# GpSimd leaves the decode and the first MLP groups; P·V takes score banks

## The chip, the cores and the metric

The kernel runs on one core of a Trainium2 chip. The metric is device time in microseconds (us) of one launch. A core has engines with instruction queues of their own that meet only through semaphores: PE (TensorE, matrix products), DVE (VectorE, elementwise work), ACT (ScalarE, activations and copies), POOL (GpSimd) and SP (SyncE, which here issues most DMAs). Each queue runs in program order, so an instruction that waits holds all that stands behind it.

## The reference

One layer of a decoder with attention and short convolution side by side, for a prompt of 512 tokens and for 8 decoded sequences of one token each. All is float32.

```python
h = rmsnorm(x); q, k, v, vc, gate_b, gate_c = split(h @ w_in)      # 2048 -> 6 x 1024
q, k = rmsnorm per head (64 wide, 16 heads)
o    = merge of 3 dilated branches (window, step) (128,1) (512,4) (2048,16), T5 bias
y    = gate_b * conv3(gate_c * vc)
x   += [rmsnorm(o) || rmsnorm(y)] @ w_out
x   += relu(rmsnorm(x) @ w_up)^2 @ w_down                          # 2048 -> 8192 -> 2048
```

For the prompt the three branches lie in the same 512 tokens and become one table of logit biases per head. For the decode a token reads a cached window of 2048 keys and values, of which 128, 96 and 96 rows (plus the new one) are used. The outputs are x of both, the new keys and values, and the rolled caches.

## The kernel before

**Numbers and layout.** The 520 tokens lie as two halves of 260 columns. A product is made from three matmuls in a reduced float32 format (fp32r): the weight's high part by x's high part, high by low, low by high. A weight tile of 128x1024 comes by DMA (`raw`), ScalarE copies its high part (`whi`, L148 or L789), VectorE subtracts for the low part (`wlo`, L149 or L790). So each weight tile needs a DMA, ScalarE and VectorE before TensorE may use it; a split is issued while the half before it is at work.

**Stages.** (1) To 36 us the first pass over x: per k-tile ScalarE and VectorE make high and low parts (`split_act`, L288 and L289) and sums of squares (L310, L311), while TensorE does the q and k of head pair 0. The bias products (L334, L335) stand ahead of it: a one-hot table by the bucket table, plus a mask `lc`. (2) To 430 us the q, k, v projections, a half of a weight column (48 matmuls) at a time. `block()` calls `step()` after every third matmul; a step advances two background generators: `norm_gen` (norm of q and k, L405 to L417) and `attn_gen` (attention of head pair j while the projections of j+1 run). (3) To 708 us the convolution's projections with `dec_gen`, the decode, as the background: a K stage (24 items of one sequence and one branch: multiply by q, reduce over the head), softmax, and a V stage (24 items: multiply by the weights, add over the branches, sum over positions by a matmul with the selector `sel`). (4) To 880 us the output projection with sums for the MLP's operands (`pair_a`, `pair_b`) and the sum of squares `acc2`. (5) To 1525 us the MLP up in 32 groups and then the MLP down in 32 groups, each group 7 products in Strassen's manner, of 24 matmuls a weight. A group's weight quarters (o, h) are combined by four sums (`SUMS`, `q_sum`), on GpSimd or VectorE as `on_vector` says. `q_prep(n)` loads, sums and splits ahead of product n; `late_gen` makes the last three operands T3, B22 and T4 while the first products run.

**PSUM banks.** Matmul outputs live in pools: `mm` for projections, `pw` (`wtile()`, 2 banks) for transposes, norms and P·V, `pS` (`stile()`, 2 banks) for scores. A pool with two banks makes the third user wait until the first is read out.

**Attention.** `products` and `score` (logits plus bias, maximum, exponential) for four blocks of queries; `norm_p` divides; `trans(hp, tb)` transposes P by TensorE (L476) into a `pw` bank, ScalarE and VectorE read it into high and low parts (L479, L480); `pv(hp)` multiplies with V (L486) into another `pw` bank and then adds two halves (L491, L492).

**What sets the order.** Every engine works in the order in which the program issues its instructions; the `wait(n)` of a generator, n steps, sets where in that order its work stands. These lines are the ones that the change touches most:

```python
P.tensor_tensor(t[:NP[g], 8 * i:8 * i + 8], ..., tiles["q", b, i][:NP[g]], OP.mult)      # K stage, L600
yield from wait(7)
V.tensor_reduce(sc[:NP[g], g, b * H:(b + 1) * H], t[:NP[g]], axis=AX.X, op=OP.add)       # L606
(V if g else P).tensor_tensor(t[:NP[g]], t[:NP[g]], w[:, :, None].to_broadcast(...), OP.mult)   # V stage, L660
T.matmul(od[m // 2], sel[:, 127 - b:255 - b], t, ...)                                    # L677
P.tensor_tensor(acc2, acc2, sq, OP.add)                                                  # L920
```

Of the kernel before, what the change touches and what calls it, by code (L numbers as in the profile page):

```python
# [25 lines left out]
F32 = mybir.dt.float32  # L26
# [58 lines left out]
def hymba_kernel(ctx, tc, xT, wi, wo, wu, wd, state_k, state_v, sconv, relb, relrep, ohp, lcp, ohd, lcd,  # L85
# [246 lines left out]
    for t in range(2):  # L332
        st = wtile()
        T.matmul(st[:H, :320], relt, oh[:, t * 320:(t + 1) * 320], start=True, stop=True)  # L334
        V.tensor_tensor(rr[:, t * 320:(t + 1) * 320], st[:H, :320], lc[:, t * 320:(t + 1) * 320], OP.add)  # L335
# [10 lines left out]
    for k in range(KT):  # L346
# [12 lines left out]
        elif k == 5:  # L359
# [3 lines left out]
            load(6)  # L363
        elif k == 9:
# [57 lines left out]
    def attn_gen(j):  # L422
# [59 lines left out]
        def pv(hp):  # L482
            st = wtile()
# [74 lines left out]
    def dec_gen():  # L558
# [36 lines left out]
        for n in range(len(items) + 1):  # L595
            if n < len(items):
                b, g = items[n]
                t = tiles["k", b, g]
                for i in range(2):
                    P.tensor_tensor(t[:NP[g], 8 * i:8 * i + 8], t[:NP[g], 8 * i:8 * i + 8],  # L600
                                    tiles["q", b, i][:NP[g]], OP.mult)
            yield from wait(7)
# [6 lines left out]
        yield from wait(6)  # L609
# [41 lines left out]
        od = [wtile(), wtile()]  # L651
# [3 lines left out]
        for n in range(len(items) + 1):  # L655
            if n < len(items):
# [3 lines left out]
                (V if g else P).tensor_tensor(t[:NP[g]], t[:NP[g]], w[:, :, None].to_broadcast([NP[g], H, E]), OP.mult)  # L660
            yield from wait(6)
            if n and items[n - 1][1]:
# [3 lines left out]
                if g == 2:  # L666
                    a = tiles.pop(("v", b, 0)).rearrange("p h e -> p (h e)")
                    parts = []
                    for i in range(2):
                        ah, al = (wk.tile([128, 512], F32R, name="ah", tag="w", bufs=16) for _ in range(2))  # L670
                        S.activation(ah, a[:, i * 512:(i + 1) * 512], AF.Copy)
                        V.tensor_tensor(al, a[:, i * 512:(i + 1) * 512], ah.bitcast(F32), OP.subtract)
                        parts += [ah, al]
                    prev(n + 2)
                    yield from wait(13)
                    for m, t in enumerate(parts):
                        T.matmul(od[m // 2], sel[:, 127 - b:255 - b], t, start=b == 0 and m % 2 == 0,  # L677
                                 stop=b == NB - 1 and m % 2 == 1)
            prev(n + 2)
            yield from wait(3)  # L680
        os = [wt((NB, 512), name="os") for _ in range(2)]
        for i in range(2):
            S.activation(os[i], od[i][:NB], AF.Copy)
        yield from wait(4)
        st = wtile()
        for f in range(8):
            T.transpose(st[:, f * NB:(f + 1) * NB], os[f // 4][:, f % 4 * 128:f % 4 * 128 + 128], ident[:NB, :NB])
        yield from wait(2)
        S.activation(R3.rearrange("p k a b -> p k (a b)")[:, :, SEQ:],
                     st[:, :64].rearrange("p (f b) -> p f b", f=8), AF.Copy)  # L690
# [113 lines left out]
    Q = {}  # L804

    def q_load(gi, o, h):
# [271 lines left out]
    for n in range(7 * NG):  # L1078
# [18 lines left out]
        if kind == "up":  # L1097
# [28 lines left out]
            if gi == 2 and pi == 4:  # L1126
# [5 lines left out]
                V.tensor_tensor(rstd2sq, rstd2, rstd2, OP.mult)  # L1132
# [123 lines left out]
```

## Time and profile before

| | us |
|---|---|
| median of 3 runs (lowest, highest) | 2200.83 (2197.87, 2202.15) |
| profiled execution, and its span | 2199.76, 2198.0 |
| PE busy | 2145.2 (98%) |
| DVE busy | 1790.6 (81%) |
| ACT busy | 965.4 (44%) |
| POOL busy | 233.3 (11%) |

The span runs from the first to the last instruction that the profiler records; 1.76 us of the profiled execution lie around it. Busy times of engines overlap, so they don't add up to the span. A row of a timeline has the start, the length in us, the engine, the line, the operation, the tile written and the tiles read with their shape, how many instructions the row stands for, and in square brackets how long the engine idled ahead of it and what ended that. "PEclk" is the granted clock of TensorE as a share of its full 2.4 GHz.

### The profile page before, as it was taken

The numbers are of one execution on the slowest core, as the hardware profiler recorded it, in microseconds if no ns is written. First come the engines' busy times: TensorE is split into PE (matmuls) and PEld (weight loads), VectorE is DVE, ScalarE is ACT, GpSimd is POOL, SyncE is SP. The second block draws the span as 40 slices with busy tenths as digits, with TensorE's granted clock in tenths as the row PEclk, the third lists the DMA queues.
The fourth block names the chain that finished last, engine by engine and source line by source line (L and its number), as shares of the span: only waits on it lengthen the run. The fifth ranks groups of instructions, "written<-read, shape, count | busy, mean of one in ns | idle before, by whom it ended". The sixth has DMA issues, their size and how long they took to land.

```text
span 2198.0 us, 42395 instructions
## 1 busy us (share of the span) xinstructions
PE 2145.2 (98%) x17568; PEld 2115.9 (96%) x17568; DVE 1790.6 (81%) x2355; ACT 965.4 (44%) x1391; POOL 233.3 (11%) x174
## 2 busy tenths in 40 slices
PE   8999999999999999899999999999999999999999
PEld 7888989998999999899999999999999999999999
DVE  6777766687787657988888888888999999999997
ACT  5444444312223334544444444445544444444443
POOL 1011010166120003630000000001100000000000
PEclk9999999999999999999999999999999999999999
DMA  5354443476544646547776676677886666666653
GB/s 197 130 171 139 170 153 111 125 219 208 169 156 160 220 171 222 202 153 243 251 247 216 235 251 232 230 254 258 319 291 246 233 247 225 237 239 247 232 195 127
DMA packets 137074, 457.75 MB, mean 208 GB/s; under 512 B 19409, under 2 KB 49745, under 8 KB 130481
## 3 DMA queue, kind: packets, MB, share of 16 engines
q1 hardware_dynamic: 136320, 454.81, 59.4%
q8 instruction: 138, 2.26, 0.4%
q14 instruction: 56, 0.45, 0.1%
q10 hardware_dynamic: 560, 0.22, 0.0%
HBM read 412.21 MB, written 181.16 MB: 270 GB/s over the span
## 4 chain that ended last, share of the span: by engine, by line
PE 85%; DVE 7%; DMA 3%; ACT 2%; issue 1%; POOL 1%; SPq 0%; DVEq 0%; ACTq 0%; POOLq 0%
PE mn L1023 28%; PE mm L1023 28%; PE mm L213 25%; DMA kv<-state_k 1%; DMA raw<-wi 1%; PE pS L453 1%; DVE wlo L790 1%; PE pw L476 1%; PE pw L486 1%; DVE wlo L149 1%; POOL kv L600 1%; DVE sc L606 1%; DVE R L790 1%; DVE raw L412 0%; PE pw L677 0%
## 5 line engine op out<-in xcount | busy, mean ns | idle before, releaser
L213 PE MATMUL mm<-R,whi 128*128 128x260 f32 x4000 | 678.1, 287 | 0.9 <-DVE R L289 0.9
L213 PEld LDWEIGHTS mm<-R,whi 128*128 128x128 f32 x4000 | 562.7, 190 | 11.6 <-issue 5.3
L1023 PE MATMUL mm<-R,whi 128*128 128x260 f32 x3008 | 549.6, 283 | 1.8 <-DVE R L790 1.2
L1023 PE MATMUL mn<-R,whi 128*128 128x260 f32 x3008 | 548.2, 283 | 0.0
L1023 PEld LDWEIGHTS mm<-R,whi 128*128 128x128 f32 x3008 | 464.9, 189 | 2.2 <-DVE R L790 1.5
L1023 PEld LDWEIGHTS mn<-R,whi 128*128 128x128 f32 x3008 | 463.7, 188 | 0.1
L1023 PE MATMUL mn<-R,wlo 128*128 128x260 f32 x1504 | 425.5, 283 | 6.3 <-DVE wlo L790 6.3
L1023 PE MATMUL mm<-R,wlo 128*128 128x260 f32 x1504 | 425.9, 283 | 5.4 <-DVE wlo L790 5.4
L213 PE MATMUL mm<-R,wlo 128*128 128x260 f32 x2000 | 404.8, 284 | 1.8 <-DVE wlo L149 1.8
L790 DVE TENSOR_TENSOR wlo<-raw,whi 128x1024 fp32r<-128x1024 f32 x255 | 319.1, 1252 | 104.9 <-ACT whi L789 103.4
L789 ACT ACTIVATE whi<-raw 128x1024 fp32r<-128x1024 f32 x255 | 269.3, 1056 | 209.6 <-PE mn L1023 95.0
L213 PEld LDWEIGHTS mm<-R,wlo 128*128 128x128 f32 x2000 | 310.7, 190 | 2.7 <-DVE wlo L149 2.2
L789 ACT ACTIVATE whi<-rg 128x1024 fp32r<-128x1024 f32 x186 | 197.3, 1061 | 219.5 <-PE mn L1023 90.1
L1023 PEld LDWEIGHTS mn<-R,wlo 128*128 128x128 f32 x1504 | 283.3, 188 | 7.8 <-DVE wlo L790 7.8
L1023 PEld LDWEIGHTS mm<-R,wlo 128*128 128x128 f32 x1504 | 284.2, 189 | 5.8 <-DVE wlo L790 5.8
L790 DVE TENSOR_TENSOR wlo<-rg,whi 128x1024 fp32r<-128x1024 f32 x186 | 230.8, 1241 | 1.7 <-ACT whi L789 1.7
L149 DVE TENSOR_TENSOR wlo<-raw,whi 128x1024 fp32r<-128x1024 f32 (+1 forms) x129 | 161.1, 1250 | 41.8 <-ACT whi L148 41.7
L148 ACT ACTIVATE whi<-raw 128x1024 fp32r<-128x1024 f32 (+1 forms) x129 | 133.5, 1038 | 128.6 <-PE mm L213 76.7
L600 POOL TENSOR_TENSOR kv<-kv,qb 128x512 f32<-128x512 f32 (+2 forms) x48 | 75.2, 1598 | 32.7 <-DMA kv<-state_k 32.7
L841 DVE TENSOR_TENSOR rg<-rg,raw 128x1024 f32<-128x1024 f32 x60 | 73.0, 1217 | 0.0
L841 DVE TENSOR_TENSOR raw<-rg,raw 128x1024 f32<-128x1024 f32 x58 | 71.1, 1225 | 2.0
L1145 DVE TENSOR_TENSOR yacc<-mm,yacc 128x520 f32<-128x520 f32 x96 | 66.6, 693 | 7.4 <-PE mm L1023 6.4
(234 smaller groups left out, 2483.2 us busy)
## 6 DMA issues: line engine op xcount, KB each, us to landing
oks<-state_k SPq DMA_DIRECT2D x184, 356.0 KB
ovs<-state_v SPq DMA_DIRECT2D x184, 356.0 KB
raw<-wi SPq DMA_DIRECT2D x94, 512.0 KB
raw<-wu SPq DMA_DIRECT2D x64, 512.0 KB
rg<-wd SPq DMA_DIRECT2D x64, 512.0 KB
raw<-wd SPq DMA_DIRECT2D x64, 512.0 KB
rg<-wu SPq DMA_DIRECT2D x60, 512.0 KB
raw<-wo SPq DMA_DIRECT2D x32, 512.0 KB
```

The source lines that it names most:

```text
L148: S.activation(his[i][:, h], raws[i][:, h], AF.Copy)
L149: V.tensor_tensor(los[i][:, h], raws[i][:, h], his[i][:, h].bitcast(F32), OP.subtract)
L213: T.matmul(ps[t][:, :HT] if isinstance(ps, tuple) else ps[:, t, :HT], a[:, k, :], b[:, t, :], start=start and n == 0, stop=stop and n == 2)
L453: T.matmul(ss[hp][:, :w], a[r, q], b[r, :w], start=n == 0, stop=n == 2)
L476: T.transpose(st[:, s * 128:(s + 1) * 128], lg[:, s * 128:(s + 1) * 128], ident)
L486: T.matmul(st[:, s * 128:], vv[:, hp, s].rearrange("p c e -> p (c e)"), b[:, s, s * 128:], start=s == 0 and n == 0, stop=s == 3 and n == 1 ...
L600: P.tensor_tensor(t[:NP[g], 8 * i:8 * i + 8], t[:NP[g], 8 * i:8 * i + 8], tiles["q", b, i][:NP[g]], OP.mult)
L789: S.activation(hi, src, AF.Copy)
L790: eng.tensor_tensor(lo, src, hi.bitcast(F32), OP.subtract)
L841: e.tensor_tensor(o_, a_, b_, op)
L1023: T.matmul(ps[:, r, :HT], a[:, k, :], b(kt), start=n % 7 in ((0, 1, 3) if kts == 8 else (0, 1)) and kt == 0 and m == 0, stop=kt == kts - 1 ...
L1145: V.tensor_tensor(dst[:, r], v[:, r], dst[:, r], OP.add)
```

## The change

Eight edits stand in it. The bias products move from ahead of the first pass into it, after tiles 7 and 8. P·V uses `stile()`. The K stage's multiplies and the V stage's g = 0 multiplies go from GpSimd to VectorE, and waits are 8 for 7, 12 for 6, and 10 for 13. The sum over positions takes the unsplit fp32 tile, in four strips of 32 PSUM partitions of one bank with 256 columns each, so `sel` is 64 wide; two 128x128 transposes follow where eight small ones did. For MLP groups 0 to 3, sum 1 is done by a DMA that adds as it writes (`accum_op`), on GpSimd's queue; the other sums of these groups, the `acc2` adds and all of `late_gen` go to VectorE, B22 in two pieces. The late squares of groups 0 to 2 become one VectorE instruction, with ScalarE's square one product later, and `rstd2sq` goes.

```diff
-    sel = cst.tile([128, 256], F32R, name="sel")
...
+    sel = cst.tile([128, 64], F32, name="sel")
+    V.memset(sel, 0.0)
+    V.memset(sel[:, 31:32], 1.0)
...
-    for t in range(2):
+
+    def bias_rows(t):
         st = wtile()
         T.matmul(st[:H, :320], relt, oh[:, t * 320:(t + 1) * 320], start=True, stop=True)
         V.tensor_tensor(rr[:, t * 320:(t + 1) * 320], st[:H, :320], lc[:, t * 320:(t + 1) * 320], OP.add)
...
+        elif k in (7, 8):
+            bias_rows(k - 7)
...
         def pv(hp):
-            st = wtile()
+            st = stile()
...
-                    P.tensor_tensor(t[:NP[g], 8 * i:8 * i + 8], t[:NP[g], 8 * i:8 * i + 8],
+                    V.tensor_tensor(t[:NP[g], 8 * i:8 * i + 8], t[:NP[g], 8 * i:8 * i + 8],
                                     tiles["q", b, i][:NP[g]], OP.mult)
-            yield from wait(7)
+            yield from wait(8)
...
-        yield from wait(6)
+        yield from wait(12)
...
-        od = [wtile(), wtile()]
+
+        od = wtile()
...
-                (V if g else P).tensor_tensor(t[:NP[g]], t[:NP[g]], w[:, :, None].to_broadcast([NP[g], H, E]), OP.mult)
+                V.tensor_tensor(t[:NP[g]], t[:NP[g]], w[:, :, None].to_broadcast([NP[g], H, E]), OP.mult)
...
-                    parts = []
-                    for i in range(2):
-                        ah, al = (wk.tile([128, 512], F32R, name="ah", tag="w", bufs=16) for _ in range(2))
-                        S.activation(ah, a[:, i * 512:(i + 1) * 512], AF.Copy)
-                        V.tensor_tensor(al, a[:, i * 512:(i + 1) * 512], ah.bitcast(F32), OP.subtract)
-                        parts += [ah, al]
+                    yield from wait(10)
+                    for c in range(4):
+                        T.matmul(od[32 * c:32 * c + 32, :256], sel[:, 31 - b:63 - b], a[:, 256 * c:256 * c + 256],
+                                 start=b == 0, stop=b == NB - 1, skip_group_check=True)
                     prev(n + 2)
-                    yield from wait(13)
-                    for m, t in enumerate(parts):
-                        T.matmul(od[m // 2], sel[:, 127 - b:255 - b], t, start=b == 0 and m % 2 == 0,
-                                 stop=b == NB - 1 and m % 2 == 1)
...
+    ADDED = 4
...
+        if (o, h) == (1, 0) and gi < ADDED:
+
+            a22 = groups[gi][3][1, 1]
+            if gi < 2:
+                for i in range(2):
+                    P.dma_start(Q[gi, o, h][i], a22[:, 4 * i:4 * i + 4], accum_op=OP.add)
+            else:
+                P.dma_start(t, a22, accum_op=OP.add)
...
-            return gi >= 4
+            return True
...
-        if gi < NG:
+        if gi < NG and not (i == 1 and gi < ADDED):
...
-            P.tensor_tensor(acc2, acc2, sq, OP.add)
+            V.tensor_tensor(acc2, acc2, sq, OP.add)
...
-        for i in range(4):
-            split2(XO["B22"][0][:, 2 * i:2 * i + 2], XO["B22"][1][:, 2 * i:2 * i + 2], R3[:, 2 * i:2 * i + 2, 1], P if i in (3,) else V)
-            yield from wait(5)
+        for i in range(2):
+            split2(XO["B22"][0][:, 4 * i:4 * i + 4], XO["B22"][1][:, 4 * i:4 * i + 4], R3[:, 4 * i:4 * i + 4, 1])
+            yield from wait(10)
...
-            split2(t4[:, 0, 2 * i:2 * i + 2], t4[:, 1, 2 * i:2 * i + 2], xs[i][:, :, 1], P if i in (1, 2, 3) else V)
+            split2(t4[:, 0, 2 * i:2 * i + 2], t4[:, 1, 2 * i:2 * i + 2], xs[i][:, :, 1])
...
         if late:
-            V.tensor_tensor(t, t, rstd2sq, OP.mult)
-        else:
-            S.activation(t, t, AF.Square)
+            V.scalar_tensor_tensor(t, t, 0.0, rstd2, op0=OP.max, op1=OP.mult)
+            relu.append(partial(square_out, t, k, n))
+            return
+        S.activation(t, t, AF.Square)
...
-                    V.scalar_tensor_tensor(t, t, 0.0, t, op0=OP.max, op1=OP.mult)
```

Three places show how the instructions move. First VectorE's queue in the decode's K stage. Before, reduces of the items (`sc<-kv`) and low parts of weights alternate:

```order
L149 TENSOR_TENSOR wlo<-raw,whi 128x1024
L606 TENSOR_REDUCE sc<-kv 97x16
L149 TENSOR_TENSOR wlo<-raw,whi 128x1024
L606 TENSOR_REDUCE sc<-kv 96x16
L700 TENSOR_TENSOR vc<-mm,rstd 128x520
L606 TENSOR_REDUCE sc<-kv 128x16
```

In the changed kernel the same stretch holds the multiplies by q as well:

```order
L149 TENSOR_TENSOR wlo<-raw,whi 128x1024
L603 TENSOR_TENSOR kv<-kv,qb 97x512 x2
L609 TENSOR_REDUCE sc<-kv 128x16
L603 TENSOR_TENSOR kv<-kv,qb 96x512 x2
L149 TENSOR_TENSOR wlo<-raw,whi 128x1024
L609 TENSOR_REDUCE sc<-kv 97x16
L603 TENSOR_TENSOR kv<-kv,qb 128x512 x2
```

Ahead of each reduce now stand two multiplies of the next item, and a weight's low part stands behind them.

Second TensorE's queue at P·V of head pair 1 (L486 before, L489 after; L476 and L479 are the transposes of the other head). Before:

```order
L486 MATMUL pw_2203<-R2_77 128x512 x2
L213 MATMUL mm_2179<-R0_75,whi_2010 128x260 x3
L486 MATMUL pw_2203<-R2_77 128x384 x2
L213 MATMUL mm_2179<-R0_75,whi_2010 128x260
L213 MATMUL mm_2179<-R0_75,wlo_2011 128x260 x2
L486 MATMUL pw_2203<-R2_77 128x256 x2
L213 MATMUL mm_2179<-R0_75,whi_2010 128x260 x3
L486 MATMUL pw_2203<-R2_77 128x128 x2
L213 MATMUL mm_2179<-R0_75,whi_2010 128x260
L213 MATMUL mm_2179<-R0_75,wlo_2011 128x260 x2
L213 MATMUL mm_2179<-R0_75,whi_2010 128x260 x3
L476 MATMUL pw_2235<-ident_114,R3_78 128x128
```

and in the changed kernel:

```order
L489 MATMUL pS_2203<-R2_77 128x512 x2
L213 MATMUL mm_2179<-R0_75,whi_2010 128x260 x3
L489 MATMUL pS_2203<-R2_77 128x384 x2
L213 MATMUL mm_2179<-R0_75,whi_2010 128x260
L213 MATMUL mm_2179<-R0_75,wlo_2011 128x260 x2
L489 MATMUL pS_2203<-R2_77 128x256 x2
L213 MATMUL mm_2179<-R0_75,whi_2010 128x260 x3
L489 MATMUL pS_2203<-R2_77 128x128 x2
L213 MATMUL mm_2179<-R0_75,whi_2010 128x260
L213 MATMUL mm_2179<-R0_75,wlo_2011 128x260 x2
L213 MATMUL mm_2179<-R0_75,whi_2010 128x260 x3
L479 MATMUL pw_2235<-ident_114,R3_78 128x128
```

The order is the same; only the bank of P·V is another, so that the transposes use both `pw` banks in turn.

Third, GpSimd's queue at the start of the MLP (`rw` and `rg` are weight quarters, `raw` too; T4x and R pieces of operands). Before:

```order
L841 TENSOR_TENSOR rw<-rw 128x512 x2
L920 TENSOR_TENSOR acc_9095<-acc_9095,sq 128x520
L841 TENSOR_TENSOR raw<-rw,raw 128x512 x2
L920 TENSOR_TENSOR acc_9095<-acc_9095,sq 128x520
L841 TENSOR_TENSOR rw<-rw,raw 128x512 x2
L841 TENSOR_TENSOR raw<-raw 128x1024
L841 TENSOR_TENSOR rw<-rw 128x512 x2
L790 TENSOR_TENSOR R_75<-R_78,R_75 128x520
L790 TENSOR_TENSOR T4x<-x_8030,T4x 128x520
```

and in the changed kernel, up to its last sums:

```order
L826 DMA rw<-wu 128x512 x4
L828 DMA rg<-wu 128x1024 x2
L848 TENSOR_TENSOR raw<-rg,raw 128x1024
L848 TENSOR_TENSOR raw<-raw 128x1024
L848 TENSOR_TENSOR rg<-rg 128x1024
```

The sums and the operand pieces are gone from this queue; six accumulating transfers stand in it, and the sums behind them belong to the end of the MLP up.

## Rows read from the trace of the kernel before

**Rows 1.** Windows: length; busy and count of PE, PEld, DVE, ACT, POOL; clock; DMA share, GB/s.

```profile
60.00:430.00 370.00, 351.98 (x2817) 332.68 (x2816) 258.89 (x621) 170.89 (x359) 33.88 (x32) 1.00 0.42 142
444.00:535.00 91.00, 89.19 (x741) 88.78 (x739) 76.51 (x66) 18.10 (x19) 69.79 (x56) 1.00 0.73 222
530.00:560.00 30.00, 25.60 (x185) 24.41 (x185) 18.22 (x24) 6.66 (x12) 8.46 (x10) 0.89 0.48 159
700.00:880.00 180.00, 180.00 (x1497) 179.88 (x1496) 123.71 (x168) 68.84 (x109) 22.75 (x17) 1.00 0.59 202
880.00:970.00 90.00, 77.47 (x599) 75.71 (x598) 81.13 (x75) 43.63 (x71) 52.81 (x24) 0.94 0.45 162
1000.00:1500.00 500.00, 500.00 (x4169) 500.00 (x4168) 418.09 (x499) 238.51 (x324) 0.00 (x0) 1.00 0.69 239
```

**Rows 2.** Waits of PE: who waits, for whom, us in total, times, longest.

```profile
PE pw L476 <- DVE R L492: 5.7, 7, 1.6
...
PE pw L476 <- DVE h L411: 5.1, 4, 1.3
```

**Rows 3.** Timeline of 0 to 10 us, all engines.

```profile
7.68 1.42 ACT L288 ACTIVATE R<-xt,g_all 128x520 fp32r<-128x520 f32 x2
...
8.79 0.88 DVE L335 TENSOR_TENSOR rr<-pw,lc 16x320 f32<-16x320 f32 x2 [6.58 <-DMA lc<-lcp]
```

**Rows 4.** Timeline of 34 to 40 us, PE.

```profile
35.95 1.58 PE L282 MATMUL pw<-acc,ones_d 128*128 128x260 f32 x6 [0.82 <-DVE acc L311]
37.17 0.83 PE L213 MATMUL mm<-R,whi 128*128 128x260 f32 x4
```

**Rows 5.** Timeline of 300 to 345 us, PE.

```profile
324.45 0.33 PE L476 MATMUL pw<-ident,R 128*128 128x128 f32 x1 [1.28 <-DVE h L411]
...
326.75 0.44 PE L476 MATMUL pw<-ident,R 128*128 128x128 f32 x2 [0.54 <-DVE R L492]
...
328.48 0.49 PE L476 MATMUL pw<-ident,R 128*128 128x128 f32 x3
```

**Rows 6.** Timeline of 312 to 336 us, DVE.

```profile
326.73 0.29 DVE L480 TENSOR_TENSOR R<-pw,R 128x128 fp32r<-128x128 f32 x1
```

**Rows 7.** Groups by line, POOL: busy us, mean ns, idle before and its releasers.

```profile
L600 POOL TENSOR_TENSOR kv<-kv,qb 128x512 f32<-128x512 f32 (+2 forms) x48 | 75.2, 1598 | 32.7 <-DMA kv<-state_k 32.7
...
L660 POOL TENSOR_TENSOR kv<-kv,pT 128x1024 f32<-128x1024 f32 x8 | 20.4, 2548 | 66.2 <-DMA kv<-state_v 37.9 <-ACT pT L642 18.0 <-DVE c L721 10.4
```

**Rows 8.** Timeline of 548 to 700 us, DVE.

```profile
567.60 1.29 DVE L672 TENSOR_TENSOR ah<-kv,ah 128x512 fp32r<-128x512 f32 x2 [0.75 <-ACT ah L671]
```

**Rows 9.** Groups by form, DVE, 444 to 535 us.

```profile
L149 DVE TENSOR_TENSOR wlo<-raw,whi 128x1024 fp32r<-128x1024 f32 x14 | 18.5, 1322 | 2.7 <-ACT whi L148 2.7
L711 DVE SCALAR_TENSOR_TENSOR y<-up,cwt,y 128x512 f32<-128x512 f32 x6 | 10.3, 1722 | 1.4 <-POOL up L705 1.2
L606 DVE TENSOR_REDUCE sc<-kv 128x16 f32<-128x1024 f32 x8 | 9.7, 1207 | 2.4 <-POOL kv L600 2.4
```

**Rows 10.** Timeline of 570 to 580 us, PE.

```profile
573.55 1.08 PE L677 MATMUL pw<-ah,sel 128*128 128x512 f32 x4
574.47 0.64 PE L213 MATMUL mm<-R,whi 128*128 128x260 f32 x4
```

**Rows 11.** Timeline of 868 to 985 us, DVE.

```profile
903.67 0.70 DVE L790 TENSOR_TENSOR T4x<-x,T4x 128x520 fp32r<-128x520 f32 x1 [1.87 <-ACT T4x L789]
...
920.46 5.70 DVE L790 TENSOR_TENSOR wlo<-rw,whi 128x512 fp32r<-128x512 f32 x2
```

**Rows 12.** Timeline of 34 to 60 us, SP.

```profile
35.92 12.47 SPq L145 DMA_DIRECT2D raw<-wi  x1
```

**Rows 13.** Timeline of 50 to 62 us, ACT.

```profile
58.05 1.06 ACT L148 ACTIVATE whi<-raw 128x1024 fp32r<-128x1024 f32 x1 [4.34 <-DMA raw<-wi]
```

**Rows 14.** Timeline of 436 to 444 us, all engines.

```profile
437.05 0.38 SPq L577 DMA_DIRECT2D kv<-state_k  x1
...
442.98 1.29 POOL L600 TENSOR_TENSOR kv<-kv,qb 96x512 f32<-96x512 f32 x1 [4.00 <-DMA kv<-state_k]
```

More of the change, by code (lines that the diff above doesn't have):

```diff
@@ L262, in hymba_kernel @@
     V.memset(ones_a, 1.0 / DA)
-    sel = cst.tile([128, 256], F32R, name="sel")
-    V.memset(sel.bitcast(F32), 0.0)
-    V.memset(sel[:, 127:128].bitcast(F32), 1.0)
+    sel = cst.tile([128, 64], F32, name="sel")
+    V.memset(sel, 0.0)
+    V.memset(sel[:, 31:32], 1.0)
     epst = cst.tile([128, 1], F32, name="epst")
@@ L667, in dec_gen @@
                     a = tiles.pop(("v", b, 0)).rearrange("p h e -> p (h e)")
-                    parts = []
-                    for i in range(2):
-                        ah, al = (wk.tile([128, 512], F32R, name="ah", tag="w", bufs=16) for _ in range(2))
-                        S.activation(ah, a[:, i * 512:(i + 1) * 512], AF.Copy)
-                        V.tensor_tensor(al, a[:, i * 512:(i + 1) * 512], ah.bitcast(F32), OP.subtract)
-                        parts += [ah, al]
+                    yield from wait(10)
+                    for c in range(4):
+                        T.matmul(od[32 * c:32 * c + 32, :256], sel[:, 31 - b:63 - b], a[:, 256 * c:256 * c + 256],
+                                 start=b == 0, stop=b == NB - 1, skip_group_check=True)
                     prev(n + 2)
-                    yield from wait(13)
-                    for m, t in enumerate(parts):
-                        T.matmul(od[m // 2], sel[:, 127 - b:255 - b], t, start=b == 0 and m % 2 == 0,
-                                 stop=b == NB - 1 and m % 2 == 1)
             prev(n + 2)
             yield from wait(3)
-        os = [wt((NB, 512), name="os") for _ in range(2)]
-        for i in range(2):
-            S.activation(os[i], od[i][:NB], AF.Copy)
+        os = wt((128, 256), name="os")
+        S.activation(os, od[:, :256], AF.Copy)
         yield from wait(4)
         st = wtile()
-        for f in range(8):
-            T.transpose(st[:, f * NB:(f + 1) * NB], os[f // 4][:, f % 4 * 128:f % 4 * 128 + 128], ident[:NB, :NB])
+        for f in range(2):
+            T.transpose(st[:, f * 128:(f + 1) * 128], os[:, f * 128:(f + 1) * 128], ident)
         yield from wait(2)
-        S.activation(R3.rearrange("p k a b -> p k (a b)")[:, :, SEQ:],
-                     st[:, :64].rearrange("p (f b) -> p f b", f=8), AF.Copy)
+        for f in range(2):
+            S.activation(R3.rearrange("p (c f) a b -> p f c (a b)", f=2)[:, f, :, SEQ:],
+                         st[:, f * 128:(f + 1) * 128].rearrange("p (c b) -> p c b", c=4)[:, :, :NB], AF.Copy)
     cp_o = cst.tile([128, 8, 2], F32, name="cp_o")
@@ L964, in late_gen @@
         for i in range(4):
-            split2(XO["T3"][0][:, 2 * i:2 * i + 2], XO["T3"][1][:, 2 * i:2 * i + 2], xs[i][:, :, 0], P if i in () else V)
+            split2(XO["T3"][0][:, 2 * i:2 * i + 2], XO["T3"][1][:, 2 * i:2 * i + 2], xs[i][:, :, 0])
             yield from wait(5)
-        for i in range(4):
-            split2(XO["B22"][0][:, 2 * i:2 * i + 2], XO["B22"][1][:, 2 * i:2 * i + 2], R3[:, 2 * i:2 * i + 2, 1], P if i in (3,) else V)
-            yield from wait(5)
+        for i in range(2):
+            split2(XO["B22"][0][:, 4 * i:4 * i + 4], XO["B22"][1][:, 4 * i:4 * i + 4], R3[:, 4 * i:4 * i + 4, 1])
+            yield from wait(10)
         t4 = cst.tile([128, 2, 8, HT], F32R, name="T4x", tag="R3")
@@ L1031, in hymba_kernel @@
     FIRST = 3
-    rstd2, rstd2sq = wt(name="rstd2"), wt(name="rstd2sq")
+    rstd2 = wt(name="rstd2")
     relu, todo, A12 = deque(), deque(), {}
@@ L1131, in hymba_kernel @@
                     rsqrt(rstd2[:, t], st[:, t, :HT], wk.tile([128, HT], F32, name="h", bufs=4))
-                V.tensor_tensor(rstd2sq, rstd2, rstd2, OP.mult)
         else:
```

## The prediction, made before the change was timed

> **What bounds the kernel.** I read the page first, then busy time by stretch, the waits of TensorE, and for each stretch that loses time the timeline of the engine that releases TensorE. TensorE is the bound: in the steady MLP it is busy for all of 500 us with 4169 matmul records, 0.12 us each [rows 1], so a product of 24 such matmuls takes 2.88 us. A stage is worth what its stretch loses against that rate: 18.0 us in the projections with attention (370 less 351.98), 1.8 in the decode's K stage (91 less 89.19), and at 530 to 560 only 185 records of 250, which is 65 x 0.12 = 7.8 us: 4.4 idle, and the rest a granted clock of 0.89, below the upper of the clock's two levels. At 880 to 970 there are 599 of 750 records, 18.1 us [rows 1]. The waits of TensorE's transposes L476 name VectorE, lines L492 and L411 [rows 2]. So the change pays where VectorE's last instruction ahead of such a wait comes earlier, and costs where its queue fills.
>
> The sum is made against the profiled run, 2199.76 us, 1.07 us below the median of 2200.83.
>
> **First pass: -2.0 us.** VectorE stands idle 6.58 us until 8.79, because the two bias adds at the head of its queue wait for the lc transfer; they take 0.88 us. ScalarE meanwhile does high parts of x (L288) from 7.68 to 9.10 [rows 3]. VectorE's work behind those adds ends late: TensorE waits 0.82 us for it at 35.95 [rows 4]. With the adds behind the seventh tile, VectorE can do low parts of x tile 0 and of the first weight halves in the idle time, some 2 to 3 us of work, and the 0.88 comes back in the pass. Bounds: 0, and -3.1 if ScalarE never holds VectorE up; the 0.88 counted, -2.0 taken.
>
> **Attention: -9.0 us.** P·V takes one of the two banks that the transposes use; the next but one transpose waits until VectorE has added the halves of P·V (L492). In each head pair from j = 3 on the trace reads as at 324.45 to 328.48: L476 waits 1.28, then 0.54, 1.8 us in all [rows 5]. The 1.28 is put down to L411, but L476 reads nothing of L411's; VectorE runs L411 to L414 ahead of L492 in one queue, and the bank is what L476 lacks. With P·V in the score banks (free by then, since all scores are done) the transposes alternate over both others. Next late is the bank of the transpose before: L480 at 326.73 ends at 327.02 [rows 6], where the transpose would be due at 328.48 - 1.82 = 326.66, so 0.36 us stays. 5 x (1.82 - 0.36) = 7.3 for j = 3 to 7. The waits for L492 come to 5.7 us [rows 2]; less five of 0.54 that leaves 3.0 in other pairs, of which I take 1.7. Bounds 0 to -10.8 (5.7 + 5.1 in full [rows 2]).
>
> **Decode, K stage: -8.0 us.** The 48 multiplies (two each for 24 items) leave GpSimd, where they take 75.2 us at 1598 ns [rows 7]. A step is three matmuls, 0.36 us, and an item 11 steps now, 3.97 us. Multiplies of this shape have no row on VectorE. Nearest: two 128x512 with two inputs take 1.29 us while GpSimd is quiet (L672) [rows 8]; beside its multiplies L711 of that width takes 1722 ns each [rows 9], 3.44 for two. GpSimd is almost empty here after the change, so 1.29. The item also holds a reduce of 1.21, its share of the splits L149 (18.5 us for 14 in 91 us, 0.81 an item) [rows 9], and about 0.65 of convolution arithmetic at quiet durations: 3.96 of 3.97. VectorE is full and just keeps up; a weight split is issued 1.6 halves of 48 matmuls, 9.2 us, ahead of its use, so a bounded lag is hidden. The wait ahead of the decode's transposes grows from 9 steps to 15, 5.4 us, which covers the last reduce. So the 1.8 and the 7.8 of the two stretches go, except some 1.6 of softmax steps there, that stay: 9.6 - 1.6 = 8.0. Bounds: -9.6, and +25 if a pair costs 3.44 (16 items inside the stretch x 2.15 = 34, less the 9.2).
>
> **Decode, V stage and sum over positions: +0.4 us.** Eight multiplies of 2548 ns [rows 7] move to VectorE, where the eight pairs of L672, 1.29 us each, go: its load hardly changes, and I count -0.4 for small waits. The sum becomes four fp32 matmuls of 256 columns into four strips of 32 partitions, for four of 512 columns that take 573.55 to 574.47, 0.92 us [rows 10]. The nearest fp32 rows are three matmuls of 260 columns, 35.95 to 37.17, 0.41 each [rows 4]. One after another: 8 x (4 x 0.41 - 0.92) = +5.8; all four at once: 8 x (0.41 - 0.92) = -4.1. No row shows strips; the middle of the two, +0.8. The Trainium skill, TensorEngine Tiling (Array Packing), Key Properties, says that different tiles work in parallel and that a change of tiling mode drains TensorE; by that the term would lie near the lower end, less sixteen drains, and no run here shows it.
>
> **Output stage: 0.** Fifteen adds into acc2 come to VectorE, 0.70 us each by another add of that width [rows 11], and now wait in its queue for ScalarE's square; 10.5 us if each reached TensorE. But TensorE is busy for all of 700 to 880, where VectorE has 123.71 us of work in 180 and GpSimd 22.75 [rows 1]: the adds fit into the rest, and contention with GpSimd ends (1722 ns against 1.29 for two [rows 8, 9]). Bounds 0 to +10.5; 0 taken.
>
> **Start of the MLP: -14.0 us.** VectorE's two 512-wide low parts at 920.46 take 5.70 us, beside GpSimd's sums [rows 11], for 1.29 quiet [rows 8]. From the last x1t to the last piece of T4 the new order puts on VectorE: three 1024-wide (at 1322 ns [rows 9], 4.0), four 512-wide (2.6), one 1024-wide sum (1.3), eight 520-wide (at 0.70, 5.6), two 1040-wide (at most 1.3 each, 2.6), seven 260-wide (at 0.43, between 0.29 for 128 [rows 6] and 0.70 for 520, 3.0) [rows 11]: 19.1 us. TensorE's five products up to T4 give 14.4, and 1.3 us of the pieces are not needed at once: 3.4 us of stall stay. Of the 18.1 lost, 0.4 is the norm's own fp32 matmuls: 18.1 - 0.4 - 3.4 = 14.3; 14.0 taken. The late squares lose six multiplies and stand behind other products. Bounds: -17.5, and 0 if as much is lost again to VectorE's fuller queue.
> The accumulating transfers have no row. Nothing from below; from above the slowest weight load of the trace, issued at 35.92 and first used at 58.05, 22.1 us [rows 12, 13], where the second sum wants it five products, 14.4 us, after the plain load: 7.7 late, in four groups +30.8. State tiles of this size land in 5.9 us (437.05 to 442.98 [rows 14]) under the same kind of load; I take 0. The Trainium skill, DMA: Bandwidth & Descriptors, Anatomy of one DMA — SWDGE (gpsimd) path, fits 2.0 us and bytes at 436 per ns; for 512 KB an estimate of 3.2 us, which leaves the sum as it is.
>
> Sum: -2.0 - 9.0 - 8.0 + 0.4 + 0 - 14.0 = -32.6; 2199.76 - 32.6 = 2167.2; with 1.07 on it, 2168.
>
> **Rivals.** *A. VectorE's queue takes over GpSimd's waits (slower).* GpSimd waits 32.7 us for K tiles and 37.9 for V tiles, 70.6 [rows 7]. The same waits at the head of VectorE's queue hold every split of weights behind them. With a lead of 9.2 us in each of two stages, 52.2 reach TensorE, and the K stage's 8.0 are not won: -24.6 + 52.2 = +27.6, 2228. It is slower than before from 24.6 + 18.4 = 43 of the 70.6 on. For it: the waits are there. Against: a tile is asked for two items, 8 us, ahead and lands in 5.9 [rows 14], and GpSimd's next buffer came free only when VectorE, slowed beside it, had reduced an earlier item. 0.07.
> *B. VectorE saturates in the K stage.* 15% over its 91 us is 13.7, less 9.2 gives +4.5, and 8.0 are not won: 2181. For it: 3.96 of 3.97. Against: L149's 1322 ns still holds contention. 0.14.
> *C. The accumulating transfers come late:* 2168 + 30.8 = 2199, as before. For it: 22.1 us has happened [rows 12, 13]. Against: 5.9 [rows 14]. 0.07. The Trainium skill, SBUF — State Buffer, Summary: rules for kernel authors, warns that a GpSimd transfer's descriptors starve while VectorE runs in its double or fourfold rate modes; by that all four would be late. VectorE's 1024 elements in 1322 ns [rows 9] do not look like such a mode.
> *D. P·V in the score banks only moves the waits:* the 1.28 and 0.54 were VectorE's queue and go over to L480 and the next L411; 9.0 are not won, 2177. For it: the page of waits names L411. 0.12.
> The forecast has 0.60.
>
> **Numbers.** Runs of this kernel tell 0.2% (4.4 us) from no change. Faster: the forecast, B, D and a little of C, 0.87; same: most of C and a mild A, 0.05; slower: A and a wider C, 0.08. The range reaches down to 2156 (the lower ends, -10.8 - 9.6 - 17.5 and 4 to 8 of the small terms) and up to 2190 (B with D, or most of the MLP's gain gone).
>
> **What would show it.** Right: no wait of L476's line for the P·V add is left; at 530 to 560 about 240 records and a clock of 1.0; VectorE over 95% busy in the K stage with TensorE still full; no pair of low parts over 2 us after 880, and one stall of some 3 us before T4. Wrong: VectorE idle for K or V tiles while TensorE waits for a split (A), TensorE waiting for splits beside a VectorE that is never idle (B), VectorE or ScalarE waiting for a GpSimd transfer at the start of the MLP (C), the transposes still late by 1.8 us per pair (D).

## The result, and the profile after

The changed kernel takes 2167.37 us (2167.03 to 2168.75), the kernel before 2199.95 (2197.87 to 2202.15): ratio 0.9853, 95% interval 0.9836 to 0.987. It is faster by 1.5%. The forecast was 2168; the sign of every large term held, though not every size, and the errors in size nearly cancel. The profiled execution has a span of 2166.0 us against 2198.0.

Busy time by stretch of the changed kernel, columns as in [rows 1] (a count stands for instruction records of the trace):

```profile
60.00:430.00 370.00, 357.80 (x2874) 339.25 (x2873) 260.52 (x623) 171.28 (x360) 33.95 (x33) 1.00 0.44 145
444.00:535.00 91.00, 91.00 (x760) 91.00 (x759) 86.03 (x113) 20.20 (x22) 2.23 (x12) 1.00 0.71 213
530.00:560.00 30.00, 29.09 (x238) 28.30 (x237) 18.41 (x27) 8.43 (x13) 0.74 (x4) 1.00 0.42 146
700.00:880.00 180.00, 177.70 (x1474) 177.00 (x1473) 120.31 (x185) 76.86 (x120) 3.67 (x4) 1.00 0.62 214
880.00:970.00 90.00, 88.48 (x735) 88.19 (x734) 74.79 (x98) 45.53 (x67) 1.72 (x2) 1.00 0.66 215
1000.00:1500.00 500.00, 500.00 (x4169) 500.00 (x4168) 418.50 (x496) 239.57 (x327) 5.38 (x2) 1.00 0.68 236
```

Against [rows 1] the K stage has lost nothing (91.00 of 91), 530 to 560 has 238 records for 185 with the clock at its upper level, and 880 to 970 has 735 for 599. GpSimd works 2.23 us where it worked 69.79. The projections still lose 12.2 us for 18.0. By 880 us the changed kernel is 19 us ahead, so equal windows are not equal work. The following landmarks mark equal work (start times in the two traces, us; the last two columns are measured and predicted changes of the stage's length):

| stage, up to | before | after | change | predicted |
|---|---|---|---|---|
| first pass, to VectorE's first scaling of a projection | 40.38 | 38.65 | -1.7 | -2.0 |
| q, k, v and attention, to the second scaling `vc` | 442.73 | 434.24 | -6.8 | -9.0 |
| rest of the convolution with decode, to the first `tmp` | 702.51 | 683.44 | -10.6 | -7.6 |
| output projection, to the first MLP matmul | 880.13 | 861.03 | 0.0 | 0 |
| MLP, to the end of the span | 2198.0 | 2166.0 | -12.9 | -14.0 |

The sum is -32.0 where -32.6 was forecast: the attention gave 2.2 less than forecast, the MLP 1.1 and the first pass 0.3 less, and the decode 3.0 more.

VectorE in the K stage (by form, as [rows 9]):

```profile
L149 DVE TENSOR_TENSOR wlo<-raw,whi 128x1024 fp32r<-128x1024 f32 x16 | 19.5, 1216 | 0.1
...
L609 DVE TENSOR_REDUCE sc<-kv 128x16 f32<-128x1024 f32 x7 | 8.5, 1210 | 0.0
...
L603 DVE TENSOR_TENSOR kv<-kv,qb 128x512 f32<-128x512 f32 x12 | 7.7, 681 | 0.0
L709 DVE SCALAR_TENSOR_TENSOR y<-up,cwt,y 128x512 f32<-128x512 f32 x6 | 4.5, 748 | 0.3
```

A multiply of 128x512, which no row of before showed, takes 681 ns, two 1.36 us against the 1.29 taken. L149 falls from 1322 to 1216 ns, the convolution's 128x512 row from 1722 to 748 ns. VectorE is busy 86.03 of 91 us there, 94.5% where over 95% was forecast: it is nearly full, TensorE waits for no weight's low part, and rival B did not come.

TensorE and VectorE around P*V of a late head pair (timelines, answering [rows 5] and [rows 6]), TensorE first:

```profile
322.64 0.55 PE L479 MATMUL pw<-ident,R 128*128 128x128 f32 x3 [0.69 <-DVE R L483]
```

```profile
321.57 0.69 DVE L495 TENSOR_TENSOR R<-pS,R 64x512 f32<-64x512 f32 x1
322.29 0.29 DVE L483 TENSOR_TENSOR R<-pw,R 128x128 fp32r<-128x128 f32 x1
```

Of the pair's two waits, 1.28 and 0.54 us [rows 5], one is left, 0.69 us. The transpose needs the bank that L483 frees at 322.29 + 0.29, and L483 stands in VectorE's queue right behind the add of P*V (L495).

### The profile page after: what moved, and what is told of

Same layout as the page of the kernel before. It is cut to its first block, busy times and chain, and to the rows that moved or that the text cites. A ratio compares the mean times of both kernels' runs of the same rounds, so it can differ in the third digit from the quotient of the medians.

```text
span 2166.0 us, 42326 instructions
## 1 busy us (share of the span) xinstructions
PE 2134.5 (99%) x17594; PEld 2105.7 (97%) x17594; DVE 1766.3 (82%) x2421; ACT 957.9 (44%) x1379; POOL 68.5 (3%) x83
## 4 chain that ended last, share of the span: by engine, by line
PE 63%; DVE 4%; ACT 1%; issue 1%; DMA 1%; DVEq 0%; SPq 0%
PE mn L1030 29%; PE mm L1030 29%; PE mm L213 5%; DVE R L788 1%; DVE wlo L149 1%; DVE wlo L788 1%; DVE x1t L934 0%; DVE acc L927 0%; DMA ra<-scr_a 0%; ACT sq L925 0%; ACT whi L148 0%; ACT x L936 0%; ACT R L936 0%; ACT R L787 0%; DMA ovs<-state_v 0%
## 5 line engine op out<-in xcount | busy, mean ns | idle before, releaser
L788 DVE TENSOR_TENSOR wlo<-raw,whi 128x1024 fp32r<-128x1024 f32 x255 | 311.9, 1223 | 109.3 <-ACT whi L787 107.5
L149 DVE TENSOR_TENSOR wlo<-raw,whi 128x1024 fp32r<-128x1024 f32 (+1 forms) x129 | 155.5, 1206 | 45.6 <-ACT whi L148 43.6
L848 DVE TENSOR_TENSOR raw<-raw 128x1024 f32<-128x1024 f32 x62 | 75.6, 1219 | 0.0
```

The costliest lines, as they stand in the source:

```text
L149: V.tensor_tensor(los[i][:, h], raws[i][:, h], his[i][:, h].bitcast(F32), OP.subtract)
L788: eng.tensor_tensor(lo, src, hi.bitcast(F32), OP.subtract)
L848: e.tensor_tensor(o_, a_, b_, op)
```

## The experiments

Times are medians; the kernel before stood at 2199.04 to 2200.23 beside them.

**P*V back in the transposes' banks.**

```diff
         def pv(hp):
-            st = stile()
+            st = wtile()
```

> The changed kernel with P*V back in the banks of the transposes (wtile), nothing else. Theory (a bank is what the transposes lacked): the two waits of L476/L479 in each of the last five head pairs come back, 1.35 us a pair by the landmarks of the two traces, so about +6.8 us, 2174; pairs 0 to 2 stay as they are, since there the wait for the P*V add only turned into one for the bank of the transpose before. Rival (the waits were VectorE's queue, and the gain of these pairs comes from elsewhere): within 2 us of 2167.

2174.40 us, +7.0 on the changed kernel, and the attention stage is 7.0 us longer in the trace. TensorE's timeline has the two waits again:

```profile
323.49 0.33 PE L479 MATMUL pw<-ident,R 128*128 128x128 f32 x1 [1.27 <-DVE h L414]
...
325.79 0.44 PE L479 MATMUL pw<-ident,R 128*128 128x128 f32 x2 [0.54 <-DVE R L495]
```

The bank was the cause of these waits; for the late head pairs rival D falls.

**The K stage's multiplies back on GpSimd.**

```diff
-                    V.tensor_tensor(t[:NP[g], 8 * i:8 * i + 8], t[:NP[g], 8 * i:8 * i + 8],
+                    P.tensor_tensor(t[:NP[g], 8 * i:8 * i + 8], t[:NP[g], 8 * i:8 * i + 8],
...
-            yield from wait(8)
+            yield from wait(7)
...
-        yield from wait(12)
+        yield from wait(6)
```

> The changed kernel with the K stage's 48 multiplies back on GpSimd and its waits of 7 and 6 steps. Theory (contention with GpSimd stretches VectorE's rows, and the stretch of the decode's transposes waits for the late reduces): +8 us, 2175, VectorE's convolution rows of 128x512 back at 1.7 us mean. Rival (the decode's gain comes from the V stage and the strips): +2 or less.

2177.85 us, +10.5, with a wide spread (2173.71 to 2179.63). Its profiled execution is the lowest of these, and there the decode is 6.0 us longer. VectorE by form, 435 to 526 us:

```profile
L149 DVE TENSOR_TENSOR wlo<-raw,whi 128x1024 fp32r<-128x1024 f32 x13 | 20.6, 1584 | 2.3 <-ACT whi L148 2.2
L709 DVE SCALAR_TENSOR_TENSOR y<-up,cwt,y 128x512 f32<-128x512 f32 x6 | 11.7, 1950 | 1.4 <-POOL up L703 1.2
```

```profile
PE mm L213 <- DVE wlo L149: 3.5, 1, 3.5
```

Rows are stretched to 1584 and 1950 ns and TensorE waits for a low part of weights, from 490.87 to 494.33 us. VectorE is busy without a gap ahead of that low part, and its longest instruction there is one of eight columns, while GpSimd does four multiplies (485.70 to 491.19):

```profile
487.47 3.75 DVE L711 SCALAR_TENSOR_TENSOR y<-sct,cwt,y 128x8 f32<-128x8 f32 x1
```

In the changed kernel the same instruction takes 0.22 us. The K stage's part is real; its size is 6 us by this trace and 10.5 by the medians.

**GpSimd busy beside the K stage, for nobody.** Three multiplies of a private tile behind each VectorE multiply:

```diff
+                    for _ in range(3):
+                        P.tensor_tensor(dm, dm, dm, OP.mult)
```

> The changed kernel, and beside each of the K stage's 48 VectorE multiplies GpSimd does three multiplies of a private tile of 192 columns with itself; nobody reads it. Theory (GpSimd's mere activity stretches VectorE's rows, and VectorE is full here): K stage rows of VectorE well over 0.69 us for 512 columns, +6 us or more. Rival (the gain came from the order and the waits of the K stage, not from contention): within 1 us of 2167.

2202.81 us, +35.4: all of the change's gain and a little more. But VectorE's waits from 430 to 560 us show a second thing:

```profile
DVE y L713 <- POOL up L707: 22.5, 2, 13.9
```

The memset of two columns of `up` is GpSimd's, and stood behind the private work. So the same run, with that memset on VectorE:

```diff
-            P.memset(up[:, 0:2], 0.0)
+            V.memset(up[:, 0:2], 0.0)
```

> The run with idle GpSimd multiplies beside the K stage cost 35 us, but its VectorE stood 14 us for the memset of up, which sat in GpSimd's queue behind the extra multiplies. Here that memset is VectorE's. Theory A (contention alone stretches rows from 0.68 to 0.79 us for 512 columns; about 0.35 us per item of 24, less the lead of 9 us): +0 to +6, 2167 to 2173. Theory B (all 35 us were contention): +30 or more.

2180.38 us, +13.0, between the two theories. The queue made 22 of the 35 us. No engine of this stage waits for GpSimd any more, so contention makes the other 13, more than A gave:

```profile
L605 DVE TENSOR_TENSOR kv<-kv,qb 128x512 f32<-128x512 f32 x14 | 11.0, 825 | 0.0
...
L713 DVE SCALAR_TENSOR_TENSOR y<-up,cwt,y 128x512 f32<-128x512 f32 x6 | 4.7, 787 | 0.1
```

```profile
PE pw L619 <- DVE sc L613: 4.1, 1, 4.1
PE mm L213 <- DVE wlo L149: 3.5, 2, 1.8
```

```profile
526.00:570.00 44.00, 36.87 (x274) 35.68 (x274) 31.75 (x42) 8.43 (x13) 40.01 (x56) 0.92 0.43 138
```

Rows of 512 columns take 0.79 to 0.83 us where they took 0.68 to 0.75, TensorE waits 4.1 us for the last reduce, and from 526 to 570, beside 7.1 us of idle time, the granted clock averages 0.92; A had left out the clock. From 435 to 570 us TensorE ends 101 records fewer than in the changed kernel, 12.1 us at 0.12 each.

**The sum over positions in its old form** (with `sel`, the wait of 13 and the eight small transposes):

```diff
-                    for c in range(4):
-                        T.matmul(od[32 * c:32 * c + 32, :256], sel[:, 31 - b:63 - b], a[:, 256 * c:256 * c + 256],
-                                 start=b == 0, stop=b == NB - 1, skip_group_check=True)
+                    for m, t in enumerate(parts):
+                        T.matmul(od[m // 2], sel[:, 127 - b:255 - b], t, start=b == 0 and m % 2 == 0,
+                                 stop=b == NB - 1 and m % 2 == 1)
```

> The changed kernel with the sum over positions in its old form: high and low parts on ScalarE and VectorE, four fp32r matmuls of 512 columns, eight small transposes, wait of 13. Theory (the strips run side by side, about 0.76 us for four against 0.92): +1.3 from the matmuls and up to 1 more from transposes and VectorE's eight pairs, 2169 to 2170. Rival (the V stage's gain is VectorE's freed time): +3 or more. Serial strips would make it faster by 6.

2172.37 us, +5.0; the decode stage is 5.4 us longer. The forecast had put the new form at +0.8, so that going back would have gained 0.8. In the changed kernel's trace the four strips are:

```profile
580.21 0.52 PE L213 MATMUL mm<-R,whi 128*128 128x260 f32 x3
580.66 0.64 PE L674 MATMUL pw<-kv,sel 128*32 128x256 f32 x8
581.23 0.39 PE L213 MATMUL mm<-R,whi 128*128 128x260 f32 x1
581.45 0.40 PE L213 MATMUL mm<-R,wlo 128*128 128x260 f32 x2
```

Three matmuls from 580.21 end their slots at 580.57; the slot of the one at 581.23 began, by the next at 581.45, at 581.33. So four strips cost 0.76 us with all that lies around them, and are issued side by side (eight records of some 390 ns in 0.64). Serial, by [rows 4], they would be 1.64. 8 x (0.92 - 0.76) = 1.3 us. In the old form the small transposes also wait for ScalarE, which they do not in the kernel before (this run first, then the kernel before):

```profile
677.66 0.89 PE L691 MATMUL pw<-ident,os 8*128 8x8 f32 x8 [2.56 <-ACT os L687]
```

```profile
685.58 0.66 PE L687 MATMUL pw<-ident,os 8*128 8x8 f32 x8
```

ScalarE's copy of `os` (677.04) stands here behind an L288 (675.88) that has waited 2.64 us for VectorE; before, the copy came at 682.71, ahead of that L288 at 695.51. After TensorE's wait the granted clock is low for a while:

```profile
680.00:685.00 5.00, 5.00 (x33) 4.94 (x31) 1.23 (x1) 0.67 (x1) 0.00 (x0) 0.74 0.49 164
```

The changed kernel has 41 to 43 records in five us there, so about 1 us goes this way. The parts come to 1.3 for the matmuls, 2.6 for the wait, 0.5 for the transposes (0.89 us against 0.38 for the two at 669.46 in the changed kernel) and 1.0 for the clock: 5.4. By its size the result is the rival's, but TensorE waits for no low part here, so VectorE's freed time isn't it. And 3.6 of the 5.4 are costs that the kernel before did not have: against that kernel the new form is worth 1.3 for the matmuls and 0.3 for the transposes (0.66 against 0.38), an estimate from these rows.

**The start of the MLP back on GpSimd** (sums, acc2, late pieces; no accumulating DMA):

```diff
-    ADDED = 4
+    ADDED = 0
...
-            return True
+            return gi >= 4
...
-            V.tensor_tensor(acc2, acc2, sq, OP.add)
+            P.tensor_tensor(acc2, acc2, sq, OP.add)
```

> The changed kernel with the start of the MLP as before: all sums of groups 0 to 3, the acc2 adds and four of the late pieces back on GpSimd, no accumulating DMA. Theory (VectorE's low parts of weights stretched beside GpSimd): +13 us, 2180, pairs of 512-wide low parts over 5 us again. Rival (the late squares' new form brought a good part): +9 or less.

2177.48 us, +10.1; the MLP is 9.1 us longer in the trace. Pairs of low parts are long again (VectorE's timeline, this run first, then a counterpart in the changed kernel):

```profile
900.14 4.51 DVE L788 TENSOR_TENSOR wlo<-rw,whi 128x512 fp32r<-128x512 f32 x2
```

```profile
880.22 1.29 DVE L788 TENSOR_TENSOR wlo<-rw,whi 128x512 fp32r<-128x512 f32 x2
```

TensorE does not wait for this pair, nor did it for the pair at 920.46 in the kernel before [rows 11]. Its longest wait here comes earlier:

```profile
877.20 0.59 PE L1030 MATMUL mm<-R,wlo 128*128 128x260 f32 x1 [3.69 <-DVE wlo L788]
```

VectorE's rows ahead of that low part are stretched too (this run, then a counterpart in the changed kernel):

```profile
872.63 1.50 DVE L788 TENSOR_TENSOR R<-R,R 128x260 fp32r<-128x260 f32 x1
```

```profile
868.16 0.42 DVE L788 TENSOR_TENSOR R<-R,R 128x260 fp32r<-128x260 f32 x1
```

TensorE waits 9.8 us in all from 855 to 1000 us, against 3.8 in the changed kernel, and the clock is 0.96 from 861 to 951 us. 7.5 of the 9.8 us are waits for VectorE, whose rows are stretched. Another part is GpSimd's own queue: ScalarE waits 4.1 us for an operand piece that GpSimd makes, and TensorE 2.3 us for ScalarE at 890.29. So contention is the larger part by the trace, but no run here divides the two, and the theory's 13 was high. The MLP's 12.9 us less these 9.1 leave 3.8 us, which the next two runs seek in the late squares.

**The late squares in the old form:**

```diff
-            V.scalar_tensor_tensor(t, t, 0.0, rstd2, op0=OP.max, op1=OP.mult)
-            relu.append(partial(square_out, t, k, n))
-            return
+            V.tensor_tensor(t, t, rstd2sq, OP.mult)
```

> The changed kernel with the late squares of groups 0 to 2 in their old form (relu times itself, then a multiply by rstd2sq on VectorE). Putting the rest of the MLP's edits back cost 9.1 us of the MLP's 12.9, so 3.8 are without an owner. Theory (the late squares' form owns them: seven more VectorE instructions of 520 columns, all in the stretch where the norm arrives): +3.8, 2171. Rival (the parts overlap, and any of them alone is worth little): +1 or less.

2167.63 us, +0.3: nothing that can be told apart. **The new form alone, on the kernel before:**

> The kernel before with the late squares' new form alone. In the changed kernel that form was worth 0.3 us, yet putting the other MLP edits back left 3.8 us of the MLP's gain. Theory (the parts overlap: with GpSimd beside it VectorE bounds the start of the MLP, and seven instructions fewer count; without it they don't): -3 to -4 us against before, 2196. Rival (those 3.8 us are something else): within 1 us of before.

2197.95 us, ratio 0.999 (0.9981 to 0.9999): 2.0 us by the medians, with an interval from 0.2 to 4.2, between the theory and its rival. Its MLP and that of the run with GpSimd back at the start of the MLP are the same code, and yet differ by 1.7 us in their traces (1315.7 and 1314.0). So the 3.8 us can be part overlap of the edits and part spread of single traces; no split is shown.

**Sum 1 of groups 0 to 3 on VectorE instead of the accumulating DMA** (`ADDED = 0` alone):

> The changed kernel without the accumulating DMAs: sum 1 of groups 0 to 3 on VectorE, 1.22 to 1.3 us each. Theory (two of the four sums fall into the stretch where VectorE is behind): +1 to +3 us, 2169. Rival (VectorE has the room, and the transfers only moved work): within 1 us.

2171.74 us, +4.4, above the theory's 3. TensorE's wait for T4 grows from 1.5 to 2.7 us, and the first 90 us of the MLP have fewer records (this run, then the changed kernel):

```profile
860.00:950.00 90.00, 84.41 (x675) 82.94 (x674) 75.56 (x101) 49.38 (x77) 0.00 (x0) 0.98 0.54 190
```

```profile
861.00:951.00 90.00, 86.18 (x707) 85.19 (x706) 74.76 (x99) 50.57 (x81) 3.48 (x4) 1.00 0.64 211
```

32 records fewer are 3.8 us: 1.8 idle and a clock of 0.98. The transfers take sums from VectorE where it is behind. In the changed kernel VectorE and ScalarE waited for none of them from 840 to 1000 us.

**The bias products ahead of the first pass:**

```diff
-        elif k in (7, 8):
-            bias_rows(k - 7)
...
+    for t in range(2):
+        bias_rows(t)
```

> The changed kernel with the two bias products ahead of the first pass again. Theory (VectorE stands behind the lc transfer and does its first pass late): +1.7 us, 2169, the first projection's scaling 1.7 us later. Rival (the first pass is bound by TensorE's start or by ScalarE): 0.

2169.27 us, +1.9, and 2.45 us at the first landmark. That is the theory's, which had +1.7.

**The add of P*V two blocks later**, behind the low part that frees a bank:

```diff
-            V.tensor_tensor(o, st[E:, :], o, OP.add)
+            later.append((o, st))
...
             trans(1, tb)
+            if tb == 1:
+                pv_add()
```

> The changed kernel with VectorE's add of the halves of P*V issued two transposed blocks later, so that it no longer stands ahead of the low part (L483) that frees the next transpose bank. Theory (the 0.69 us left in each of the last five head pairs is L483 queued behind that add): -3.5 for these and up to -1.2 for pairs 0 and 1, 2163. Rival (what is left is the latency of transpose, ScalarE's copy and VectorE): 0.

2165.14 us (2163.50 to 2165.64), ratio 0.984 (0.9825 to 0.9855): 2.2 us below the changed kernel by the medians, 4.1 in the attention stage by the traces. No transpose waits from 200 to 430 us any more. It has the lowest median of all kernels run; its four times lie below the changed kernel's four, though the intervals of the two ratios overlap.

**The same, with GpSimd's part of q's and k's squares on VectorE too:**

```diff
-            P.tensor_tensor(sq, raw, raw, OP.mult)
-            P.tensor_tensor(sl_, sq, sh.bitcast(F32), OP.subtract)
+            V.tensor_tensor(sq, raw, raw, OP.mult)
+            V.tensor_tensor(sl_, sq, sh.bitcast(F32), OP.subtract)
```

> The kernel with the late P*V add, and with the two GpSimd instructions per q and k projection (square of raw, and its low part) on VectorE too. Theory (in pairs 0 to 2 the transposes wait 1.16 us each because the division L473 takes 1.15 us beside GpSimd against 0.42): these waits of about 4 us shrink, 2161 against 2165 for the late add alone. Rival (VectorE's 1.4 us more per projection delays the norms that the same stretch waits for): 2165 or more.

2166.59 us, 1.5 above the late add alone: the theory falls. In the late add's kernel GpSimd is idle around the first of these waits (its work ends at 81.03), and the division takes 0.49 us; around the second the division takes 1.34 beside GpSimd's work. Both transposes wait the same, 1.17 and 1.16 us, and without GpSimd's work 1.17 each. VectorE in the late add's kernel, then TensorE's first wait:

```profile
85.51 0.49 DVE L477 TENSOR_SCALAR lg<-lg,sm 128x512 f32<-128x512 f32 x1
...
87.33 0.43 DVE L417 SCALAR_TENSOR_TENSOR raw<-h,raw 128x260 f32<-128x260 f32 x1
87.67 0.55 DVE L487 TENSOR_TENSOR R<-pw,R 128x384 fp32r<-128x384 f32 x1
...
129.93 1.34 DVE L477 TENSOR_SCALAR lg<-lg,sm 128x512 f32<-128x512 f32 x1
```

```profile
88.28 0.66 PE L483 MATMUL pw<-ident,lg 128*128 128x128 f32 x4 [1.17 <-DVE R L487]
```

The 128x384 low part that frees the bank stands behind four instructions of the norm, L414 to L417 (86.13 to 87.67). That is the order of one queue, not contention. What the run adds is four new waits of 0.61 to 0.65 us for such low parts, from 222 to 359 us, as its rival said of VectorE's longer queue.

## Why the prediction came out

The large terms came out by the mechanisms that were forecast. That the sum is within 0.6 us is in part luck: the forecast had 3.6 us too much gain in three stages and 3.0 too little in the decode.

**First pass, -2.0.** Right: -1.7, and putting it back costs 1.9. VectorE's first low part starts at 4.75 us, not behind an add at 8.79 [rows 3]:

```profile
4.75 0.76 DVE L289 SCALAR_TENSOR_TENSOR R<-xt,g_all,R 128x520 fp32r<-128x520 f32 x1 [2.75 <-ACT R L288]
```

**Attention, -9.0.** The mechanism was right, shown by putting the bank back; the size was not: -6.8. Three pieces failed. The residual was read from VectorE's row as 0.36 us [rows 6]; it is 0.69 to 0.70, because the add of P*V and the low part stay in one queue, whatever bank they read, and the late add shows it. The last of the five pairs did not read like the others; it had a single wait:

```profile
419.72 0.44 PE L476 MATMUL pw<-ident,lg 128*128 128x128 f32 x2 [1.58 <-DVE R L492]
```

So the five pairs waited 8.8 us before, not 9.1, and wait 3.0 now: 5.8 for the 7.3 forecast. And the 1.7 us for pairs 0 to 2 did not come but for 0.2; the larger of the two waits for L492 there (before, then now):

```profile
187.81 0.44 PE L476 MATMUL pw<-ident,R 128*128 128x128 f32 x2 [1.36 <-DVE R L492]
```

```profile
187.80 0.55 PE L479 MATMUL pw<-ident,R 128*128 128x128 f32 x3 [1.26 <-DVE R L483]
```

The waits there passed on to the next bank, which is rival D's mechanism at two places:

```profile
PE pw L479 <- DVE R L483: 9.1, 11, 1.3
```

9.1 us, where the same line of before had 4.3.

**Decode, -7.6 in all.** -10.6. Up to one and the same scaling of `vc` in the V stage (VectorE, before, then now)

```profile
594.30 0.70 DVE L700 TENSOR_TENSOR vc<-mm,rstd 128x520 f32<-128x520 f32 x1 [0.86 <-PE mm L213]
```

```profile
576.07 0.70 DVE L698 TENSOR_TENSOR vc<-mm,rstd 128x520 f32<-128x520 f32 x1 [1.36 <-PE mm L213]
```

the decode has gained 9.7 us from its start at 442.73 and 434.24. Of these 0.9 is a sum over positions that the changed kernel does only behind this place. So the K stage with its softmax gave about 8.8, an estimate, for the 8.0 forecast, and the run with its multiplies on GpSimd loses 6 to 10.5. The cause is contention: GpSimd's work for nobody brings the loss back. The rest of the stage gave about 1.8 where 0.4 more was forecast. The term that failed is the sum over positions: +0.8, taken between serial (+5.8) and side by side (-4.1), where the rows give -1.3 for the matmuls and -0.3 for the transposes. The sign was wrong, though the bounds held. Strips work side by side here, as the Trainium skill, TensorEngine Tiling (Array Packing), Key Properties, says of tiles; the trace's 0.76 us for four agrees, against 1.64 one after another. It is 0.35 more than one alone; whether that is the drain of which the page speaks, no run tells. The 5.0 us that the old form costs in the changed kernel are no measure of this term, since most of them are a wait and a clock that the kernel before did not have.

**Output stage, 0.** 177.62 and 177.59 us: right.

**MLP, -14.0.** -12.9. One stall of 3.4 us before T4 was forecast; TensorE's waits at the start are four, and the one for T4 is the last:

```profile
870.58 0.39 PE L1030 MATMUL mm<-R,wlo 128*128 128x260 f32 x1 [0.38 <-DVE wlo L788]
...
874.71 0.51 PE L1030 MATMUL mm<-R,whi 128*128 128x260 f32 x2 [1.22 <-ACT cs L1113]
...
878.80 0.39 PE L1030 MATMUL mn<-R,wlo 128*128 128x260 f32 x1 [0.70 <-DVE wlo L788]
...
883.22 0.48 PE L1030 MATMUL mm<-T4x,whi 128*128 128x260 f32 x2 [1.52 <-DVE cs L1117]
```

0.38 + 1.22 + 0.70 + 1.52 = 3.8 us, 0.4 more than forecast; the other 0.7 us has no row of its own. No pair of 512-wide low parts takes over 2 us after 880 any more, as forecast. The late squares, counted inside, are worth nothing measurable in this kernel.

**Rivals.** A: VectorE waits 1.1 us in all for V tiles and never for a K tile from 430 to 700 us, so GpSimd's 70.6 us [rows 7] did not pass on. That they were waits for buffers that VectorE freed late is argued, not shown. C: neither VectorE nor ScalarE waited for an accumulating transfer in the stretch named; the six landed 7.5 us after their issue by the median, for the 5.9 taken. The Trainium skill, SBUF — State Buffer, Summary: rules for kernel authors, says that a GpSimd transfer's descriptors starve while VectorE is in its double or fourfold mode. No such effect shows here, beside VectorE's rows of 1.22 us for 1024 elements.

## What to carry to other kernels

An engine that helps at 11% of the time can cost more than it gives: price its work by what it does to the rows of the engine beside it, then look for instructions of the critical engines that stand behind its queue. When a wait for a bank is removed, the next candidate is the instruction queued just behind the one removed; move that too, or count only a part (here 5.8 us of 8.8 went). Terms whose only rows are far apart need a run of their own: here the one small term taken in the middle, +0.8, had the wrong sign. And an edit that is put back into the changed kernel is priced in that kernel: the old sum over positions cost 5.0 us there, most of it by a wait that the kernel before never had.

## What the runs showed that was not expected

- Four fp32 matmuls of 256 columns with 32 output partitions each, in four strips, take 0.76 us in all between other matmuls; three of 260 columns over the whole array take 0.41 each [rows 4].
- GpSimd's multiplies of only 192 columns on a private tile stretch VectorE's two-input rows from 0.68 to between 0.77 and 0.83 us; the reduce of one input stays at 1.20 to 1.21. The Trainium skill, SBUF — State Buffer, Who interferes with whom, says just this: an instruction with two inputs in SBUF shares a read port with GpSimd, a reduce never does. The rows agree. With the kernel's own multiplies of 512 columns the same kind of row went to 1.72 [rows 9] and 1.95 us, and one row of eight columns to 3.75 for 0.22.
- A two-column memset in the helper's queue cost VectorE 22.5 us of waiting in two waits once that queue was full.
